# A hybrid encoder trunk on one core: float32 value and band products on halves of the array, and a new order of the head groups

## The chip, the cores and the metric

The kernel runs on one core of one Trainium2 chip. Its time is the device time of one execution in microseconds. The core has a matrix engine (TensorE; PE in the profile, its weight loads PEld), VectorE (DVE), ScalarE (ACT), GpSimd (POOL), and a queue that issues DMAs (SyncE, SP). TensorE reads SBUF and writes its results into PSUM, eight banks of 128 partitions x 512 float32.

## The reference

The input is x, 1024 tokens of 1024 channels in float32. Two layers are computed. Each normalises x, projects it with one matrix, and splits the columns among four groups of attention heads. Per layer:

```python
h = rms_norm(x, norm1_g[l])
proj = h @ w_in[l]
(a_cq, a_ckv, a_kr, b_q, b_k, b_v, c_q, c_k, c_v, d_q, d_k, d_v) = jnp.split(proj, splits, axis=-1)
y_a = mla_mixer(...)    # A: 4 heads, dense, keys of 64 + 32, from a low-rank latent
y_b = diff_mixer(...)   # B: 4 heads, dense, two softmaxes of keys of 32, p0 - lam * p1
y_c = swa_mixer(...)    # C: 4 query heads, 2 key heads of 64, keys within 128 tokens, with a sink
y_d = na_mixer(...)     # D: 4 heads of 64, a neighbourhood of 8 rows x 16 columns of the token grid
mix = jnp.concatenate([rms_norm(y_a), y_b, rms_norm(y_c), rms_norm(y_d)], axis=-1)   # gains left out here
x = x + mix @ w_out[l]
h = rms_norm(x, norm2_g[l])
x = x + jnp.square(jax.nn.relu(h @ w_up[l])) @ w_down[l]
```

After the layers x is normalised once more. All is float32, and so are the products as far as rounding goes: the kernel makes a float32 product out of three faster ones (below).

## The kernel before, in words

**Layout.** Everything is kept transposed: a tile has 128 channels on the partitions and the 1024 tokens along the row. Tokens go in halves of 512, a PSUM bank each.

**Split products.** A float32 operand is split into a high part, rounded to the reduced format float32r (ScalarE copies it, line 196), and a low part, the rest (a subtraction on VectorE or GpSimd, line 190). A product is then high x high + high x low + low x high, three matmuls in float32r (`passes`, lines 222 to 224). A projection of 128 channels is 2 halves x 8 blocks of inputs x 3 = 48 such matmuls.

**Stages of a layer** (`attention`, line 381). Two waves of projections make B's queries, keys and values (`several`, line 232). Then main streams of attention run, each with a fill beside it. `weave` (line 545) takes steps of the main stream and puts fill steps between them at a ratio; the main stream is emitted with a priority `lead`. The main streams and fills are, in order:

- B (`attn_b`, 871), with the latent projections of A and the projections of D as fill;
- D (`attn_d`, 1035), with the projections of C and the second, low-rank projections of A (`latent_up`, 698) as fill;
- C (`attn_c`, 1068), then A (`attn_a`, 931), both with the first half of the output projection for four of its eight tiles as fill (`groups_bd`, 472);
- the rest of the output projection (505 to 538).

Then comes the MLP (`mlp`, 1144), with an order of its own on TensorE; the change doesn't touch it. Queries, keys and values go through DRAM between projection and attention, written and read on SP's queue. A scheduler puts the emitted instructions of the attention stages in order on each engine, by its own model of durations and by the priorities; each engine then works strictly in that order.

**Dense attention** (A and B: `softmax`, 803, and `dense`, 818). For 128 queries: scores against all keys (line 810; B's three split passes are stacked along the contraction, 96 rows, and A needs three matmuls), a minimum on VectorE (812), exp on ScalarE (815). B combines two such tiles: a scaled copy on ScalarE (898) and a sum on GpSimd (899). For two query tiles at a time the probabilities are transposed on TensorE, four 128 x 128 blocks to a bank (846), and split into `pth` (ScalarE) and `ptl` (VectorE). The value product (834, 835) has as weights a tile of 64 high and 64 low channels of v, so that the upper half of the output is added to the lower one at the end (`pv_out`, 749). Per 128 keys there are two matmuls of 256 columns, one for `pth`, one for `ptl`.

**Banded attention** (C and D: `banded`, 966), one head at a time. Each of 8 query tiles meets the three key tiles around it. The score product is two matmuls in float32r over 128 rows, on which high and low parts are stacked (982). VectorE adds bias or mask and takes the minimum (1058, 1089), ScalarE takes exp (1061, 1092). Up to three blocks are transposed (991), split, and multiplied with v (1003, 1004), into a bank that was zeroed by a product (1032).

**After a group**: denominators are inverted, transposed, and sent through DRAM so that each row of a tile gets them (`denominators`, 761); the group is normalised and split for the output projection (`mix_b`, `mix_group`). These tails are generators; `tick` (774) takes a step of them now and then.

**Places.** In the attention stages PSUM is divided as mm 2 (products and small things), tr 2 (transposes), sb 3 (scores), pv 1 (value products); in the output projection all eight banks are mm.

Of the kernel before, what the change touches and what calls it, by code (L numbers as in the profile page):

```python
# [14 lines left out]
F = mybir.dt.float32  # L15
# [85 lines left out]
def layout(i):  # L101

    def padded(a, axis):
# [9 lines left out]
    wo = i["w_out"].reshape(n, 8, P, DM)[:, [2, 3, 6, 7, 4, 5, 0, 1]].reshape(n, DM, DM)  # L113
# [23 lines left out]
        + [col(i["out_g_" + s]) for s in ("mla", "swa", "na")]  # L137
# [10 lines left out]
class Trunk:  # L148
    def __init__(self, ctx, tc, d, out):
        self.ctx, self.tc, self.nc, self.d, self.out = ctx, tc, tc.nc, d, out  # L150
        self.ahead, self.tails = 4, deque()
# [117 lines left out]
    def rows_of(self, col, grid=False):  # L269

        n = col.shape[1]
        ps = self.bank("mm", [n, P])
        self.nc.tensor.transpose(ps, col, self.ident)
        sb = self.cp.tile([n, P], F, tag="rows", name="rows")
        self.nc.vector.tensor_copy(sb, ps)
        dr = self.dram.tile([n, P], F, tag="rows", bufs=4, name="drows")
        if grid:
            flat = dr.rearrange("a b -> (a b)").rearrange("(r b c) -> b r c", r=16, b=8)
            self.store(flat, sb.rearrange("b (r c) -> b r c", r=16))
        else:  # L280
            self.store(dr, sb)
        return dr
# [98 lines left out]
    def attention(self, l):  # L381
# [8 lines left out]
        qb, kb, vb = dr([2, 2, 4, 16, 2, S], "qb"), dr([2, 2, 4, 16, 2, S], "kb"), dr([4, P, 8, P], "vb")  # L390
        qd, kd, vd = dr([2, 2, P, S], "qd"), dr([2, 2, P, S], "kd"), dr([4, P, 8, P], "vd")
        qc, kc, vc = dr([2, 2, 2, 32, 2, S], "qc"), dr([2, 2, 32, 2, S], "kc"), dr([2, P, 8, P], "vc")
        lat, krd = dr([2, 3, P, S], "lat"), dr([2, 16, 2, S], "krd")
        qa = dr([2, 2, P, S], "qan"), dr([2, 4, 16, 2, S], "qar")
        ka, va = dr([2, 2, P, S], "kan"), dr([4, P, 8, P], "va")
# [13 lines left out]
        def proj_d():  # L409
            for t in range(2):  # L410
                yield from one(T_DQ[t], xs, self.ev_grid(rb, self.to_parts(qd[:, t], 0.125)))
                yield from one(T_DK[t], xs, self.ev_grid(rb, self.to_parts(kd[:, t])))
                yield from one(T_DV[t], xs, self.ev_grid(rb, self.to_values(vd[2 * t:2 * t + 2])))

        def proj_c():
            tabs = self.table("64", rb, nc.gpsimd)
            for t in range(2):
                yield from one(T_CQ2[t], xs, self.ev_rope(tabs, qc[:, t]))
            yield from one(T_CK, xs, self.ev_rope(tabs, kc))
# [4 lines left out]
        with ExitStack() as stack, ExitStack() as att:  # L424
            self.ap = att.enter_context(sbuf("att"))
            with self.banks(mm=2, tr=2, sb=3, pv=1):
                with sbuf("proj", "right") as self.pp:
# [35 lines left out]
                    self.tails.append(self.mix_b(mix, y["b"], self.gsub[:, l:l + 1]))  # L463
                    fill = chain(proj_c(), self.latent_up(l, lat, rows, qa, ka, va))
                    self.weave(self.attn_d(l, qd, kd, vd, y["d"]), fill, self.RD, self.LD, every=self.EV[1])
                gout = lambda n: self.gout[n][:, l]
                self.tails.append(self.mix_group(mix, 2, y["d"], gout("na")))
                wa = stack.enter_context(sbuf("wa", "right"))
                wo = stack.enter_context(sbuf("wo", "right"))
                sums, w_out = [], d["w_out"][l]  # L470

                def groups_bd():

                    for m in range(self.EARLY):
                        x = wo.tile([P, S], F, tag="sum", bufs=self.EARLY, name="sum")
                        self.load(x, saved[m])
                        sums.append(x)
                    while None in mix[:4]:
                        yield True
                    for m, x in enumerate(sums):  # L480
                        ws = self.weights(w_out[m, 0])
                        for n in range(2):
                            ps = self.mm_ps()
                            self.product(ps, ws, mix[:4], n)
                            sl = slice(n * 512, n * 512 + 512)
                            self.tt(x[:, sl], ps, x[:, sl], ALU.add)
                            yield True

                fill = groups_bd()
# [3 lines left out]
                self.tails.append(self.mix_group(mix, 6, y["a"], gout("mla"), nc.vector))  # L493
            with self.banks(mm=8):
# [9 lines left out]

                while None in mix[:6]:
# [84 lines left out]
    def ev_rope(self, tabs, dst):  # L590

        dst = dst.rearrange("a g f h s -> a (g f) h s")

        def ev(n, ps):
# [7 lines left out]
            self.emit_parts(t1, [(dst[:, :, h, sl].rearrange("a p s -> p a s"), slice(h * 64, h * 64 + 64))  # L602
                                 for h in range(2)])
# [30 lines left out]

    def to_values(self, dst, tag="mm"):
# [3 lines left out]
        def then(n, y):  # L639
# [3 lines left out]
            src = ps.rearrange("p (k h d) -> p h k d", k=4, h=2)  # L643
            b = self.both()
            v = b.rearrange("p h (k e) -> p h k e", k=4)
# [853 lines left out]
```

## Time and profile before

| | us |
|---|---|
| median of the 3 runs shown (lowest, highest) | 2697.52 (2692.25, 2699.81) |
| the profiled execution | 2692.41 |
| its span, from first to last instruction | 2690.6 |
| TensorE busy in it | 2545.8 |
| VectorE busy | 2014.2 |
| ScalarE busy | 1442.9 |
| GpSimd busy | 496.9 |

How to read it: an instruction group is named by the line of code that emits it, engine, operation, and out<-in by the program's own tile names. Lines 190 and 196 are those of the helpers that split, so there the tile names tell what is meant: `wl<-raw,wh` is a low half of weights, `ptl<-tr,pth` one of probabilities. A matmul's record lasts longer than its slot: the next one starts before it ends. Spacings of starts are therefore the price of a matmul in a stream, and durations its latency. PEclk is the share of its clock that TensorE was granted. In the table by stage, the figures behind "PE", "DVE" and so on are busy microseconds with the number of instructions, then the granted clock, the busy share of the DMA engines and GB/s.

### The profile page before, as it was taken

Reading aid. Unit: us, or ns where it says so; the run is one execution under the profiler, and the core shown is the slowest. Engines: PE = TensorE matmul, PEld = TensorE weight load, DVE = VectorE, ACT = ScalarE, POOL = GpSimd, SP = SyncE. Lnnn points to the kernel's source line nnn. Section 1 sums busy time; section 2 is a strip of 40 time slices with the busy share of each in tenths; the row PEclk is TensorE's granted clock in tenths of the full one; section 3 lists DMA queues with packets and bytes.
Section 4 is the critical chain, followed back from the end, with each engine's and each line's share of the span. In section 5 each row is a group of like instructions: output and inputs, shape, how many; then the busy total and the mean of one; then the engine's idle time right before and its main releaser. Section 6 shows DMA issues by size and latency. Waiting matters only on the chain.

```text
span 2690.6 us, 36835 instructions
## 1 busy us (share of the span) xinstructions
PE 2545.8 (95%) x12296; PEld 2107.6 (78%) x12296; DVE 2014.2 (75%) x3827; ACT 1442.9 (54%) x2601; POOL 496.9 (18%) x306
## 2 busy tenths in 40 slices
PE   8989988999899999999999999789998999999997
PEld 7778876787778887888877788678887788778886
DVE  6777867774977778888668777677749677788886
ACT  4667757664534444444437777576635344444444
POOL 2555642201000000000035556331010000000000
PEclk9999989999999999999999999889999999999998
DMA  5533598322144447444244446962221444664431
GB/s 169 177 106 123 160 282 254 83 88 60 51 154 143 161 162 269 146 141 141 96 136 140 121 118 174 306 200 70 70 71 61 152 152 151 227 221 150 132 102 63
DMA packets 186927, 389.15 MB, mean 145 GB/s; under 512 B 23712, under 2 KB 26736, under 8 KB 186736
## 3 DMA queue, kind: packets, MB, share of 16 engines
q1 hardware_dynamic: 172912, 361.62, 43.7%
q10 hardware_dynamic: 13824, 25.17, 2.6%
q8 instruction: 97, 1.59, 0.2%
q14 instruction: 94, 0.77, 0.1%
HBM read 263.29 MB, written 123.41 MB: 144 GB/s over the span
## 4 chain that ended last, share of the span: by engine, by line
PE 74%; DVE 12%; DMA 6%; ACT 4%; issue 3%; POOL 1%; SPq 0%; DVEq 0%; ACTq 0%; POOLq 0%
PE u L222 8%; PE u L224 8%; PE u L223 8%; PE mm L222 5%; PE mm L223 5%; PE mm L224 5%; PE p L222 5%; PE p L223 5%; PE p L224 5%; PE sb L810 3%; PE tr L846 2%; DVE p L812 2%; DVE part L190 2%; PE pv L835 2%; PE pv L834 2%
## 5 line engine op out<-in xcount | busy, mean ns | idle before, releaser
L196 ACT ACTIVATE wh<-raw 128x512 fp32r<-128x512 f32 x448 | 281.8, 630 | 595.9 <-PE u L223 336.0
L190 DVE TENSOR_TENSOR wl<-raw,wh 128x512 fp32r<-128x512 f32 x448 | 306.8, 685 | 76.9 <-ACT wh L196 75.6
L190 POOL TENSOR_TENSOR wl<-ws,wh 128x512 fp32r<-128x512 f32 (+1 forms) x112 | 146.5, 1310 | 1107.0 <-DMA saved<-x 664.1
L224 PE MATMUL u<-far,wl 128*128 128x512 f32 x768 | 302.4, 394 | 6.2 <-DVE wl L190 6.0
L222 PE MATMUL u<-far,wh 128*128 128x512 f32 x768 | 302.4, 394 | 3.3 <-ACT ev L1251 2.1
L223 PE MATMUL u<-far,wh 128*128 128x512 f32 x768 | 301.8, 393 | 0.9 <-DVE far L190 0.9
L190 DVE TENSOR_TENSOR ptl<-tr,pth 128x512 fp32r<-128x512 f32 (+2 forms) x384 | 238.3, 629 | 67.5 <-ACT pth L196 65.8
L815 ACT ACTIVATE p<-p,nm 128x1024 f32<-128x1024 f32 x192 | 220.1, 1147 | 91.1 <-DVE nm L812 89.6
L196 ACT ACTIVATE pth<-tr 128x512 fp32r<-128x512 f32 (+2 forms) x384 | 204.9, 546 | 104.4 <-PE tr L846 55.8
L222 PE MATMUL p<-far,wh 128*128 128x512 f32 x640 | 251.2, 393 | 2.6 <-DVE ev L190 2.6
L224 PE MATMUL p<-far,wl 128*128 128x512 f32 x640 | 250.0, 391 | 2.9 <-DVE wl L190 2.9
L223 PE MATMUL p<-far,wh 128*128 128x512 f32 x640 | 250.3, 391 | 0.0
L810 PE MATMUL sb<-stack 96*128 96x512 f32 x640 | 217.6, 421 | 18.8 <-DVE nm L812 17.8
L190 POOL TENSOR_TENSOR p<-p 128x1024 f32<-128x1024 f32 x64 | 154.0, 2410 | 141.4 <-ACT p L898 132.1
L190 DVE TENSOR_TENSOR raw<-raw 128x512 f32<-128x512 f32 x256 | 174.6, 686 | 6.7 <-DMA raw<-in_w_up 2.0
L224 PEld LDWEIGHTS u<-far,wl 128*128 128x128 f32 x768 | 145.8, 190 | 38.4 <-DVE wl L190 7.9
L222 PEld LDWEIGHTS u<-far,wh 128*128 128x128 f32 x768 | 146.1, 190 | 35.3 <-ACT ev L1251 2.9
L223 PEld LDWEIGHTS u<-far,wh 128*128 128x128 f32 x768 | 145.8, 190 | 31.9 <-DVE far L190 1.6
L222 PE MATMUL mm<-xh,wh 128*128 128x512 f32 x416 | 168.9, 406 | 1.3 <-DVE part L190 0.7
L812 DVE CUSTOM_DVE_ANT_0 p<-sb,zero,nm 128x512 f32<-128x512 f32 x192 | 142.4, 742 | 32.2 <-PE sb L810 28.6
L224 PE MATMUL mm<-xh,wl 128*128 128x512 f32 x416 | 166.5, 400 | 0.0
L223 PE MATMUL mm<-xl,wh 128*128 128x512 f32 x416 | 166.4, 400 | 0.0
(245 smaller groups left out, 5993.1 us busy)
## 6 DMA issues: line engine op xcount, KB each, us to landing
act<-acts SPq DMA_DIRECT2D x224, 256.0 KB
raw<-in_w_up SPq DMA_DIRECT2D x128, 256.0 KB
acts<-ev SPq DMA_DIRECT2D x128, 256.0 KB
raw<-in_w_down SPq DMA_DIRECT2D x128, 256.0 KB
acts<-ev ACTq DMA_DIRECT2D x96, 256.0 KB
ws<-in_w_in SPq DMA_DIRECT2D x76, 256.0 KB
rz<-drows SPq DMA_DIRECT2D x40, 256.0 KB
stack<-kd SPq DMA_DIRECT2D x32, 256.0 KB
```

What stands on the lines that cost most here:

```text
L190: (eng or self.nc.vector).tensor_tensor(out=out, in0=a, in1=b, op=op)
L196: nc.scalar.activation(hi, src, AF.Copy)
L222: mm(ps, w[0], x[0][:, sl], start=start, stop=False)
L223: mm(ps, w[0], x[1][:, sl], start=False, stop=False)
L224: mm(ps, w[1], x[0][:, sl], start=False, stop=stop)
L810: self.nc.tensor.matmul(ps, q[:, qt * P:(qt + 1) * P], k[:, sl], start=i == 0, stop=i == len(passes) - 1)
L812: self.nc.vector.tensor_tensor_reduce(out=p[:, sl], in0=ps, in1=self.zero[:, 0:1].bitcast(F).broadcast_to([P, 512]), scale=-scale, scalar= ...
L815: self.nc.scalar.activation(p, p, AF.Exp, bias=nm[:, 1:2], scale=-1.0, accum_out=z)
L834: nc.tensor.matmul(out, v[:, kt], h[:, sl], start=kt == 0, stop=False)
L835: nc.tensor.matmul(out, v[:, kt], lo[:, sl], start=False, stop=kt == 7)
L846: nc.tensor.transpose(t[:, k * 256 + i * P:k * 256 + (i + 1) * P], p[:, (j * 2 + k) * P:(j * 2 + k + 1) * P], self.ident)
```

## The change

**Value products in float32.** The transposed probabilities are copied once out of PSUM, unsplit, by ScalarE; in the stage of A and the bands ScalarE and VectorE take turns. v is kept as plain float32, 64 channels. A dense value product has 64 output rows: for even key tiles it writes partitions 0 to 63, for odd ones 64 to 127, and `pv_out` adds the halves as before. The eight products of a group of 256 queries are emitted in one go, after all four transposed tiles.

**Banded attention in float32, two heads at a time.** Two heads are stacked on the 128 partitions. Scores of one head use rows 0 to 63 of the array, those of the other rows 64 to 127; value products write 64 output rows each. Product results need no addition: one ScalarE copy takes them out (`pair_out`). C's key head and query head are paired anew, for which the host reorders C's rows of `w_out` and gains.

**B's combination** becomes one VectorE operation in place of ScalarE's copy and GpSimd's sum.

**Normalisation** of two heads shares one transpose and one way through DRAM (`normalise`).

**Order.** All projections, C's and A's second ones included, are fill beside B. Then A is the main stream, and D and C, in turn, its fill, with PSUM as mm 1, tr 2, sb 3, pv 2. The output projection stands whole after that.

```diff
-                    fill = chain(self.proj_latent(l, one, xs, rb, tabs, lat, krd, rows), proj_d())
+                    fill = chain(self.proj_latent(l, one, xs, rb, tabs, lat, krd, rows), proj_d(), proj_c(),
+                                 self.latent_up(l, lat, rows, qa, ka, va))
                     self.weave(chain.from_iterable(self.attn_b(l, t, qb, kb, vb, y["b"]) for t in range(2)),
                                fill, self.RB, self.LB, every=self.EV[0])
-                    fill = chain(proj_c(), self.latent_up(l, lat, rows, qa, ka, va))
-                    self.weave(self.attn_d(l, qd, kd, vd, y["d"]), fill, self.RD, self.LD, every=self.EV[1])
...
+            def bands():
+                yield from self.attn_d(l, qd, kd, vd, y["d"])
                 self.tails.append(self.mix_group(mix, 2, y["d"], gout("na")))
...
-                self.weave(self.attn_c(l, qc, kc, vc, y["c"]), fill, self.RC, end=False, every=self.EV[2])
+                yield from self.attn_c(l, qc, kc, vc, y["c"])
                 self.tails.append(self.mix_group(mix, 4, y["c"], gout("swa")))
-                self.weave(self.attn_a(l, qa, ka, krd, va, y["a"]), fill, self.RA, self.LA, every=self.EV[3])
+            self.turns = (True, False)
+            with self.banks(mm=1, tr=2, sb=3, pv=2), sbuf("band", "right") as self.bp:
+                self.weave(self.attn_a(l, qa, ka, krd, va, y["a"]), bands(), self.RA, self.LA, every=self.EV[1])
...
-    EV = (.5, .5, .7, 1)
-    EARLY, RC, RA, LA = 4, (8, 1), (3, 1), 0
+    EV = (.5, 1)
+    EARLY, RA, LA = 4, (17, 42), 40
-    NP, RB, RD, LB, LD = 6, (7, 8), (3, 2), 40, 50
+    NP, RB, LB = 6, (18, 41), 40
...
         def step(job, j):
...
-            h, lo = self.transposed(512)
-            self.split(h, lo, t)
-            ready.append((job, j, h, lo))
-            if len(ready) > 1:
-                product(*ready.pop(0))
+            ready.append(self.transposed(t))
+            if j == 3:
+                runs.append((job, list(ready)))
+                ready.clear()
+
+        def products():
+            job, pts = runs.pop(0)
+            probs, g, v, y, half, done = job
+            if g % 2 == 0:
+                self.pv = self.bank("pv")
+            out = self.pv[:, (g % 2) * 256:(g % 2) * 256 + 256]
+            for n, j in enumerate((3, 2, 1, 0)):
+                for k in range(2):
+                    nc.tensor.matmul(out[k * 64:(k + 1) * 64], v[:, j * 2 + k], pts[j][:, k * 256:k * 256 + 256],
+                                     start=n == 0, stop=n == 3)
...
+    def transposed(self, ps, pool=None, tag="pt", bufs=None):
+        t = (pool or self.ap).tile([P, 384 if pool else 512], F, tag=tag, bufs=bufs or self.NT, name="pt")
+        t = t[:, :ps.shape[1]]
+        if self.turns[0]:
+            self.nc.vector.tensor_copy(t, ps)
+        else:
+            self.nc.scalar.activation(t, ps, AF.Copy)
+        self.turns = self.turns[::-1]
+        return t
...
-                nc.scalar.activation(ps[1], ps[1], AF.Copy, scale=c)
-                self.tt(ps[0], ps[0], ps[1], ALU.add, nc.gpsimd)
+                nc.vector.scalar_tensor_tensor(out=ps[0], in0=ps[1], scalar=c, in1=ps[0], op0=ALU.mult, op1=ALU.add)
...
         def score(i):
...
-            for n, k in enumerate(ks):
-                mm(ps, qs[:, i * P:(i + 1) * P], k[:, keys], start=n == 0, stop=n == 1)
+            ps = [self.bank("sb")[:, :w] for _ in heads]
+            for b, r in zip(ps, heads):
+                mm(b, q[r, i * P:(i + 1) * P], k[r, lo * P:(hi + 1) * P], start=True, stop=True)
...
+        def products(pv, half, kbs):
+            for kb in kbs:
+                pts, i0, i1 = done[kb]
+                q0, q1 = max(i0, half * 4), min(i1, half * 4 + 3) + 1
+                for r, v, pt in zip(heads, vs, pts):
+                    mm(pv[r, (q0 - half * 4) * P:(q1 - half * 4) * P], v[:, kb], pt[:, (q0 - i0) * P:(q1 - i0) * P],
+                       start=False, stop=kb == 2 + 3 * half)
```

The helper functions that only carry data in the new layouts (`to_rows`, `to_values`, `vtile`, `ev_rope` with `whole`, the head loops of `attn_c` and `attn_d`) change with it and are not shown. `ahead`, the number of query tiles whose scores a band computes in advance, goes from 4 to 2.

More of the change, by code (lines that the diff above doesn't have):

```diff
@@ L469, in attention @@
[L469 to L487, printed above, removed]
@@ L765, in denominators @@
         yield
[L766 removed]
+        rz = self.rz_tile()
+        for j in range(2):
+            self.spread(rz[j * 64:(j + 1) * 64], rows, j, 2)
         yield
[L769 removed]
         self.tt(y, y, rz, eng=eng or self.nc.gpsimd)
@@ L867, in dense @@
             step(job, j)
-        product(*ready.pop(0))
+        while runs:
+            products()
         yield True
```

332 lines of the change are left out of this document (162 added, 170 removed).

## The prediction

> **What bounds the kernel now.** I read the page from the top: busy times, slices, chain.
>
> ```profile
> span 2690.6 us, 36835 instructions
> ...
> PE 2545.8 (95%) x12296; PEld 2107.6 (78%) x12296; DVE 2014.2 (75%) x3827; ACT 1442.9 (54%) x2601; POOL 496.9 (18%) x306
> ...
> PE   8989988999899999999999999789998999999997
> ...
> PEclk9999989999999999999999999889999999999998
> ...
> PE 74%; DVE 12%; DMA 6%; ACT 4%; issue 3%; POOL 1%; SPq 0%; DVEq 0%; ACTq 0%; POOLq 0%
> ```
>
> TensorE is busy 95% of the span and holds 74% of the chain: this is a TensorE kernel. Its few holes are places where the PE slice falls to 7 or 8 and the clock row drops with it. So I cut the span into stages (busy time by stage). Layer 0 runs from 0 to 696, its MLP to 1365, layer 1 from there to 2026. In each layer the rows are: first projections, B, D, C, then A with the output projection.
>
> ```profile
> core 0: us, PE busy (x) PEld busy (x) DVE busy (x) ACT busy (x) POOL busy (x), PEclk, DMA share, GB/s
> 0.00:109.00 109.00, 96.97 (x409) 78.16 (x410) 75.91 (x111) 50.49 (x78) 40.15 (x31) 0.94 0.61 196
> 109.00:330.00 221.00, 211.66 (x1152) 178.44 (x1151) 169.02 (x433) 161.65 (x263) 125.96 (x71) 0.98 0.41 119
> 330.00:415.00 85.00, 74.72 (x401) 63.58 (x400) 55.32 (x143) 53.33 (x132) 36.63 (x24) 0.90 0.97 287
> 415.00:509.00 94.00, 80.87 (x429) 62.66 (x428) 68.75 (x180) 64.28 (x155) 20.89 (x13) 0.96 0.56 173
> 509.00:696.00 187.00, 181.96 (x1031) 154.64 (x1032) 124.89 (x248) 102.59 (x180) 24.20 (x19) 1.00 0.26 75
> ...
> 1365.00:1437.00 72.00, 66.59 (x273) 53.28 (x272) 49.51 (x72) 28.21 (x49) 29.43 (x20) 0.91 0.62 179
> 1437.00:1651.00 214.00, 206.73 (x1131) 174.45 (x1129) 163.73 (x429) 160.64 (x261) 124.97 (x70) 0.98 0.41 119
> 1651.00:1740.00 89.00, 74.87 (x413) 64.76 (x410) 56.60 (x143) 53.66 (x132) 38.73 (x26) 0.92 0.97 281
> 1740.00:1838.00 98.00, 86.06 (x437) 68.92 (x436) 73.29 (x183) 64.93 (x157) 21.12 (x12) 0.88 0.55 170
> 1838.00:2026.00 188.00, 182.31 (x1033) 155.01 (x1034) 125.87 (x249) 102.99 (x181) 25.06 (x19) 1.00 0.25 74
> ```
>
> In the B and the A rows TensorE is idle for 3 to 4%. In the four D and C rows it is idle for 49.5 us (10.3, 13.1, 14.1, 11.9), 12 to 16% of each, and its clock is 0.88 to 0.96 there. D's row also has the DMA engines at 0.97, and the chain there runs over the latent loads:
>
> ```profile
> 1683.74 7.15 DMA rq<-drows
> 1690.91 9.87 DMA latp<-lat
> ```
>
> So there are two things to price: whether TensorE gets more or less to do, and whether those holes close.
>
> **TensorE's own work.** The pace of the present forms, from the spacing of starts in the order of time:
>
> ```profile
> 303.56 0.29 PE L834 MATMUL pv<-pth,v 128*128 128x256 f32 x1
> 303.68 0.28 PE L835 MATMUL pv<-ptl,v 128*128 128x256 f32 x1
> ...
> 305.09 0.39 PE L224 MATMUL mm<-xh,wl 128*128 128x512 f32 x1
> 305.32 0.39 PE L222 MATMUL mm<-xh,wh 128*128 128x512 f32 x1
> ...
> 35.76 1.95 PE L299 MATMUL mm<-ident,rs_r 128*128 128x128 f32 x16
> 37.46 0.48 PE L222 MATMUL pv<-xh,wh 128*128 128x512 f32 x1
> ...
> 1870.39 0.46 PEld L846 LDWEIGHTS tr<-ident,p 128*128 128x128 f32 x4
> ...
> L299 PE MATMUL mm<-ident,rs_r x64: 270/275/421, 35.8 to 2073.7; 128*128 128x128 f32 x64
> ...
> L1004 PE MATMUL pv<-ptl,v x160: 223/337/687, 365.0 to 1835.9; 128*128 128x256 f32 x64, 128*128 128x384 f32 x64, 128*128 128x128 f32 x32
> ```
>
> A split (float32r) product of 512 columns takes a slot of 0.23 us, one of 256 columns 0.117; on that line 384 columns are 0.172 and 128 are 0.062. L299 is the only plain float32 product with many columns: its 8 instructions leave 16 records, so each is two passes, and 16 in 1.70 us is 0.106 a pass. Is that the price of 128 columns, or of the weight load beside them? One pass lasts 270 ns at least; the split product of as many columns (L1004's shortest) lasts 223. The extra 47 ns is about one 128-column stream (0.055), so I read two cycles a column: a float32 instruction of 256 columns takes 0.424 alone, 384 takes 0.636, 128 takes 0.212. The lower bound (0.106 is the load alone) would be half of it.
>
> Removed, in both layers: 1024 value products of B and A, 1024 x 0.117 = 120; the bands' 320 value products, 128 x 0.172 + 128 x 0.117 + 64 x 0.062 = 41; the bands' scores, 192 x 0.172 + 64 x 0.117 = 40; 16 zeroing products, 4. Together 205 us.
>
> Added: 512 float32 value products, 217; the bands' 64, 64 and 32, 75; the bands' 128 scores, 75. Together 366 us if each runs alone, 183 if two always run side by side on the halves of the array (64 output rows each, or 64 input rows each). No run of before has two products on halves, so the pairing is a bound from both sides. I take pairing in order: the second pass of one instruction beside the first pass of the next. Then each unbroken run leaves one pass uncovered. In the changed program's order the 672 stand in 216 runs (58 full eights, but 44 lone scores: the scheduler puts transposes between). 216 x 0.27 = 59, so 183 + 59 = 242: **37 us more** than the 205 removed. By this term alone the change loses; gain can only come from the holes.
>
> **The other engines.** These rows carry the terms:
>
> ```profile
> L190 DVE TENSOR_TENSOR ptl<-tr,pth 128x512 fp32r<-128x512 f32 x256 | 173.2, 685 | 43.0 <-ACT pth L196 42.2
> L190 DVE TENSOR_TENSOR ptl<-tr,pth 128x384 fp32r<-128x384 f32 x96 | 52.0, 550 | 17.3 <-ACT pth L196 16.4
> L196 ACT ACTIVATE pth<-tr 128x512 fp32r<-128x512 f32 x256 | 148.0, 590 | 59.5 <-PE tr L846 55.8 <-DVE ptl L190 1.8 <-PE pv L834 0.2
> L898 ACT ACTIVATE p<-p,cb 128x1024 f32<-128x1024 f32 x64 | 72.9, 1144 | 12.2 <-DVE cb L897 10.3 <-DVE cb L896 0.8 <-DVE rs_r L255 0.7
> L190 POOL TENSOR_TENSOR p<-p 128x1024 f32<-128x1024 f32 x64 | 154.0, 2410 | 141.4 <-ACT p L898 132.1 <-PE mm L224 4.4 <-PE mm L222 4.0
> L200 DVE SCALAR_TENSOR_TENSOR xl<-x,par,xh 128x1024 fp32r<-128x1024 f32 x16 | 24.4, 1529 | 7.6 <-ACT xh L199 7.6
> L190 DVE TENSOR_TENSOR part<-mm,tabs 64x512 f32<-64x512 f32 x32 | 22.0, 688 | 0.5
> L190 DVE TENSOR_TENSOR part<-mm,tabc 128x512 f32<-128x512 f32 x16 | 11.0, 686 | 7.2 <-PE mm L224 3.9 <-PE mm L726 3.3
> L190 DVE TENSOR_TENSOR part<-mm,rkv 128x512 f32<-128x512 f32 x16 | 10.9, 683 | 2.2 <-PE mm L224 1.4 <-POOL both L190 0.7
> ```
>
> The low half on VectorE goes, 225 us and the step after the ScalarE copy with it (1.28 us per transposed tile become 0.6). B's scaled copy (1.14) and GpSimd sum (2.41) become one VectorE operation, at 1.53 by L200: 98 us. In stage A half the copies go to VectorE, 0.69 each for 64 and at most 0.55 for 64 banded ones: 79. VectorE loses 225 - 98 - 79 = 48 us net, ScalarE 73 and half of A's copies. GpSimd's B row loses 77 of its 126 us and takes on the low halves of the moved weights. One denominator transpose and DRAM trip now serves two heads, and values, D's and C's queries and keys go through DRAM once and not as two halves. None of these was on the path: TensorE's B row is 97% busy beside them. I count nothing for them; if TensorE should wait for VectorE in the new A stage, that is in the 11% below.
>
> **The stages, layer 1.** First projections: 72, unchanged. B takes over from D's row C's four projection tiles, 192 x 0.227 = 44, and the latent ones, 54 x 0.227 = 12, with some 24 transposes, 2: 58 us more on TensorE. Their weight loads, the latent loads and the stores go along on SP's queue, out of a row with the DMA engines at 0.97 into one at 0.41, so the 17 us of latent loads find other products in front. B: 214 + 58 = 272.
>
> A with D and C: A's scores 192 x 0.227 = 44, 432 transposes at a slot of 0.109 (0.46 us for four weight loads) 47, the float32 products 242/2 less B's 31 = 90, the rest 7: 188 us on TensorE. VectorE has 256 us in the D, C and A rows now; less 44 and 26 of low halves, plus 39 of copies, less the evacuations that move to B (the last three rows of the last fence, 44 in both layers, so 22) and the output's 24 sums at 0.69 (16), it has near 187 in the A stage and the output together, some 175 of it in the stage. ScalarE (222 in the three rows, less the same copies) stays below. So TensorE is first, VectorE close behind, and **the cover is gone**: up to now independent projections stood beside every group (D and C still lost 12 to 16%, A beside the output projection 3%); now A and the bands have only each other. A product that waits at the head of TensorE's queue holds the other group's transposes too, and with two transpose banks for both, the VectorE and ScalarE copies behind. I take a loss of 11%, between the A row and the D and C rows: 208.
>
> Output projection: 384 x 0.227 = 87, alone, plus 8 for the hand-over, 95. A's tail runs beside the first 240 of these products (54 us), so it costs nothing unless it is longer than they are.
>
> Sum: 72 + 272 + 208 + 95 = 647 against 661. Layer 0: 109 + 279 + 208 + 95 = 691 against 696. The MLP is untouched. Together -19 us on the profiled execution, which took 2692.4 us, 1.8 beyond its span and 5 below the median of the runs shown: **2674 us**. With the A row's 3% loss it would be 2644, with D's 16% 2704; that is the forecast's own range, both signs in it.
>
> **Rivals.**
>
> (1) *The halves don't overlap* (ends slower). Then the float32 products take 366, not 242: 124 us more, 23 of it in each B stage, 39 in each A stage. TensorE would have 227 us in stage A, far ahead of the other engines, so of the loss there only some 13 remain in place of 20: 2674 + 124 - 14, and 12 less for B's present idle time (17 us in both layers), = 2772. For it: no row shows any overlap. Against it: no row either. It ends slower than before as soon as a fifth of the second passes stays uncovered (the 18 us of gain are a fifth of the 98 between the two cases). The Trainium skill (TensorE: Matmul & The Clock Gate, section on packing small matmuls) gives 2.38 times for three column tiles; by it the 366 would be about 230. No run here shows that.
>
> (2) *Each change between halves and whole array waits for the array to empty.* A 512-column product lasts 0.39 while the next starts after 0.23: 0.16 us are normally hidden. The 216 runs have some 420 edges; 0.16 each is 67 us, none of it hidden by another engine: 2741. For it: 44 lone scores between transposes. Against it: only that no trace has such an edge. The Trainium skill (TensorEngine Tiling (Array Packing), Key Properties) says that changing the mode drains TensorE; by that rule this rival is the time. No row here can say.
>
> (3) *Both passes of a pair run side by side and the holes close.* Then 183, no uncovered pass, and A's 3%: 2644 - 59 = 2585, and with half of that 2615. Faster.
>
> (4) *The change doesn't do what it says*: A waits for the latent values at the hand-over from B, since they are now the last of the fill, the way D's row waited for 17 us. 17 us in each layer: 2708.
>
> **How the numbers follow.** Forecast 0.42, (1) 0.27, (2) 0.15, (3) 0.10, (4) 0.06. About 0.3% (8 us) is what a measurement can tell from no change. The forecast's range gives 0.30 faster, 0.06 same, 0.06 slower; (3) is faster; (1) and (2) slower; (4) 0.02 same, 0.04 slower. Faster 0.40, same 0.08, slower 0.52. The range reaches over (4) and (2) to just past (1), and down to the half-way case of (3): 2612 to 2776. It leaves out half of (3) and the upper half of what (1) could be.
>
> **What would show it.** In the new trace the float32 value products start every 0.21 us per instruction inside a run of eight (forecast), every 0.42 (rival 1), or 0.11 (rival 3). The first start after a run comes 0.16 us late under rival 2. The A stage is near 208 us with TensorE above 85% and VectorE next. B lasts about 275 with TensorE at 95% or more, and no DMA chain at its end. Wrong would be: B bound by VectorE's new sums, or TensorE's clock below 0.9 through stage A.

## The result, and the profile after

The changed kernel takes **2741.07 us** (2735.18 to 2745.17), the kernel before 2698.22 beside it: ratio 1.0161, interval 1.0137 to 1.0186, so 43 us slower. The forecast was 2674, on the faster side. First the page of the changed kernel: span, busy times, the slices of TensorE and of its clock.

```profile
span 2739.3 us, 35471 instructions
...
PE 2599.4 (95%) x12264; PEld 2000.2 (73%) x12264; DVE 1892.8 (69%) x3531; ACT 1296.2 (47%) x2373; POOL 325.5 (12%) x222
...
PE   8999989998989998999999998999999999999997
...
PEclk9999999998999999999999999999999999999998
```

The other engines got lighter, as intended: VectorE by 121 us, ScalarE by 147, GpSimd by 171. TensorE got heavier by 54, and it was already the bound. The 7 inside the row of slices, where D's group stood in layer 1, is gone and the clock dips less often; yet the time went up. Cut into stages (rows: first projections, B, A with the bands, output projection, MLP; then layer 1 and its MLP):

```profile
0.00:112.00 112.00, 96.13 (x403) 76.41 (x404) 75.02 (x115) 50.21 (x78) 33.87 (x28) 0.94 0.58 178
112.00:395.00 283.00, 268.37 (x1368) 198.96 (x1367) 181.41 (x420) 145.55 (x260) 85.05 (x59) 0.97 0.45 134
395.00:609.00 214.00, 206.85 (x1189) 129.51 (x1187) 123.34 (x347) 124.83 (x285) 9.47 (x4) 0.98 0.28 80
609.00:723.00 114.00, 103.76 (x441) 82.95 (x440) 53.00 (x81) 38.00 (x68) 34.38 (x23) 0.91 0.28 82
723.00:1390.00 667.00, 648.36 (x2852) 532.59 (x2852) 526.84 (x815) 300.33 (x504) 9.75 (x6) 0.99 0.45 146
1390.00:1466.00 76.00, 68.49 (x270) 52.73 (x269) 50.33 (x79) 28.47 (x50) 23.87 (x18) 0.89 0.57 163
1466.00:1750.00 284.00, 267.81 (x1370) 197.78 (x1369) 180.92 (x419) 145.59 (x260) 85.79 (x59) 0.98 0.45 134
1750.00:1965.00 215.00, 207.46 (x1194) 130.14 (x1192) 123.78 (x348) 124.78 (x286) 9.46 (x4) 0.98 0.28 80
1965.00:2073.00 108.00, 98.84 (x440) 79.98 (x441) 53.72 (x81) 38.12 (x68) 33.89 (x23) 0.95 0.26 81
```

| stage, layer 0 / layer 1 | forecast | measured |
|---|---|---|
| first projections | 109 / 72 | 112 / 76 |
| B and all projections | 279 / 272 | 283 / 284 |
| A and the bands | 208 / 208 | 214 / 215 |
| output projection | 95 / 95 | 114 / 108 |

Two things are to be seen. The stage of A and the bands is nearly right in length, but for another reason: TensorE is busy 207 of its 214 us (97%), where the forecast had 188 of 208. And the output projection, 384 products that need 87 us, is the stage that is furthest off, with a clock of 0.91.

**Inside the A stage.** A part of TensorE's order of time in that stage; a float32 instruction leaves two records, so x16 is a run of eight products, x2 a single half.

```profile
480.27 1.94 PE L872 MATMUL pv<-pt,v 128*64 128x256 f32 x14
482.14 0.66 PE L857 MATMUL tr<-ident,p 128*128 128x128 f32 x4
482.73 0.65 PE L872 MATMUL pv<-pt,v 128*64 128x256 f32 x2
483.30 0.66 PE L857 MATMUL tr<-ident,p 128*128 128x128 f32 x4
...
487.56 1.95 PE L872 MATMUL pv<-pt,v 128*64 128x256 f32 x16
489.44 0.76 PE L1014 MATMUL tr<-ident,p 128*128 128x128 f32 x5
```

From its start to the start behind it the run of eight takes 1.88 us. In experiment 1, where the eight stand one after the other, it takes 3.60; so the halves do run side by side. In the single records of this trace the two halves of a pair start 0.007 us apart and the next pair 0.209 later. The price is at the ends: four transposes between two groups of halves take 0.59 (482.14 to 482.73) where four slots of 0.109 are 0.44, and the lone half takes 0.57 where its two passes are 0.43. That is **0.15 us for each change between halves and whole array** (0.094 before the first instruction of the new mode and 0.052 behind it, in the records). The trace has 418 changes of mode, 14 of them between the two kinds of halves (64 output rows, 64 input rows), which cost as much: 418 x 0.146 = 61 us. Without them the products and scores on halves take 241 us in all.

**Inside the output stage.** The rows of one tile (duration min/median/max, first and last start) and then stretches of that stage, 609 to 618 and on:

```profile
L193 POOL TENSOR_TENSOR yd<-yd,rz x4: 2342/2408/2417, 545.6 to 621.0; 128x1024 f32<-128x1024 f32 x4
...
L369 ACT ACTIVATE sq<-yd x2: 1043/1044/1046, 549.8 to 553.8; 128x1024 f32<-128x1024 f32 x2
```

```profile
609.00:618.00 9.00, 7.76 (x33) 6.40 (x32) 1.68 (x6) 1.28 (x4) 0.00 (x0) 0.63 0.32 89
618.00:639.00 21.00, 16.38 (x66) 12.05 (x65) 9.92 (x13) 5.58 (x8) 10.36 (x5) 0.91 0.25 64
639.00:652.00 13.00, 11.33 (x46) 9.36 (x47) 3.58 (x8) 2.80 (x8) 5.82 (x6) 0.75 0.21 63
652.00:668.00 16.00, 13.54 (x54) 10.24 (x54) 5.80 (x6) 5.51 (x8) 6.93 (x5) 0.94 0.38 91
668.00:723.00 55.00, 54.75 (x246) 44.90 (x245) 32.02 (x49) 22.83 (x41) 11.27 (x10) 0.99 0.27 89
```

D's group was squared by 555 and then lay still for some 60 us: the last of its products on GpSimd starts at 621.0, after the A stage. The tails advance by one step (a tick) for each step of A, A has 17 steps, and D's, C's and B's remaining tails want more than that. So D's last, C's whole and A's tail run one behind the other in the output stage. Until 668 TensorE is busy 49 of 59 us at a clock between 0.63 and 0.94; then it runs full.

### The profile page after: what moved, and what is told of

It reads as the page before. It is cut to its first block, busy times and chain, and to the rows that moved or that the text cites. A ratio compares the mean times of both kernels' runs of the same rounds, so it can differ in the third digit from the quotient of the medians.

```text
span 2739.3 us, 35471 instructions
## 1 busy us (share of the span) xinstructions
PE 2599.4 (95%) x12264; PEld 2000.2 (73%) x12264; DVE 1892.8 (69%) x3531; ACT 1296.2 (47%) x2373; POOL 325.5 (12%) x222
## 5 line engine op out<-in xcount | busy, mean ns | idle before, releaser
L193 POOL TENSOR_TENSOR wl<-ws,wh 128x512 fp32r<-128x512 f32 (+1 forms) x112 | 156.1, 1397 | 1061.6 <-ACT wh L199 1013.7
L823 ACT ACTIVATE pt<-tr 128x512 f32<-128x512 f32 (+2 forms) x256 | 140.0, 558 | 164.0 <-PE tr L857 99.3
L857 PE MATMUL tr<-ident,p 128*128 128x128 f32 x1024 | 168.2, 281 | 14.9 <-DVE p L926 9.5
L857 PEld LDWEIGHTS tr<-ident,p 128*128 128x128 f32 x1024 | 121.2, 142 | 65.5 <-issue 18.9
```

Of the source, the lines that this page charges most:

```text
L193: (eng or self.nc.vector).tensor_tensor(out=out, in0=a, in1=b, op=op)
L823: self.nc.scalar.activation(t, ps, AF.Copy)
L857: nc.tensor.transpose(t[:, k * 256 + i * P:k * 256 + (i + 1) * P], p[:, (j * 2 + k) * P:(j * 2 + k + 1) * P], self.ident)
```

## The experiments

Ratios are to the kernel before, with the 95% interval.

| version | us | ratio |
|---|---|---|
| the change | 2741.07 | 1.0161 [1.0137, 1.0186] |
| all products on one half | 2821.78 | 1.0452 [1.0429, 1.0474] |
| runs of two | 2786.44 | 1.0318 [1.0291, 1.0345] |
| runs kept whole, nothing else | 2729.93 | 1.0136 [1.0116, 1.0156] |
| tails early | 2700.84 | 1.0005 [0.9995, 1.0016] |
| order alone, split products | 2816.43 | 1.0431 [1.0415, 1.0447] |
| order alone, tails early | 2777.01 | 1.0293 [1.0269, 1.0317] |
| dense float32 products, B's combination and normalisation, old order | 2711.95 | 1.0051 [1.0032, 1.0070] |
| tails early, bands split | 2695.67 | 0.9997 [0.9985, 1.0010] |
| tails early, even fill | 2749.84 | 1.0196 [1.0181, 1.0211] |
| tails early, bands split, even fill | 2752.65 | 1.0208 [1.0194, 1.0222] |
| tails early, runs kept whole | 2693.65 | 0.9978 [0.9965, 0.9992] |
| tails early, runs whole, even fill | 2722.83 | 1.0088 [1.0065, 1.0111] |
| tails early, runs whole, bands split, even fill | 2717.27 | 1.0069 [1.0046, 1.0091] |
| tails early, runs whole, bands split | 2694.54 | 0.9990 [0.9980, 1.0000] |

**1. Do the halves overlap?** All dense products go to one half.

```diff
-out[k * 64:(k + 1) * 64], ..., start=n == 0, stop=n == 3
+out[0:64], ..., start=n == 0 and k == 0, stop=n == 3 and k == 1
```

> Edit of the changed kernel: all eight dense value products of a run write the same 64 output rows, so that two can never be side by side; the addition of the halves goes. Theory (TensorE bounds B and A, and the halves overlap fully: in the changed kernel's trace two products start 6 ns apart and the next two 209 ns later): 512 products take 0.427 us in place of 0.213, +109 us, some 10 of it into idle time: 2835 to 2850. Rival (the new A stage is bound by its softmax chain, and the overlap is worth little): under +40, below 2780.

Measured +81 us against the change, less than the 94 to 109 expected and far above the rival. The row is seven products, for which the change has 1.94:

```profile
483.92 3.24 PE L870 MATMUL pv<-pt,v 128*64 128x256 f32 x14
```

The overlap is real: without it the change would have lost 123 us, not 43.

**2. What does a change of mode cost?** The pair of products is put behind each block of transposes; the same products, but 699 changes of mode in place of 419.

```diff
-            if j == 3:
-                runs.append((job, list(ready)))
+            if len(ready) > 1:
+                products()      # one pair
```

> Edit of the changed kernel: each pair of dense value products is emitted after the transposes of the next pair, as before, and not in runs of eight. In the order of instructions the changes between half and whole array go from 419 to 699. Theory (each such change waits until the array is empty, 0.094 us more than a start in a stream, and nothing hides it): +26 us, 2762 to 2772. Rival (the changes cost nothing that counts; what costs is the order of the groups): within 8 us of 2741.

Measured +45 us, above the range: the expectation knew of 0.094 for each of the 280 changes, and the 0.146 read above gives 41. The trace also has 29 more halves that stand alone, which at 0.22 each are another 6.

**3. Are the tails the loss in the output stage?**

```diff
-    EV = (.5, 1)
+    EV = (.5, 3)
```

> Edit of the changed kernel: three steps of the groups' tails for every step of stage A in place of one. In the changed kernel D's and C's normalisations end only after A, in the output projection, where TensorE idles for 10 us a layer and runs at a lower clock. Theory (the output projection waits for these tails): the output stage of 114 and 108 us comes near 95, so -25 to -30 us, 2711 to 2720. Rival (it waits for its own weights, or the tails take the same time from stage A): within 8 us of 2741.

Measured -40 us: this one number brings the change back to the time before. The output row of this version, and its D tile:

```profile
606.00:703.00 97.00, 94.34 (x435) 76.42 (x435) 48.24 (x72) 33.98 (x61) 24.12 (x19) 1.00 0.24 74
```

```profile
L193 POOL TENSOR_TENSOR yd<-yd,rz x2: 2362/2364/2365, 515.2 to 517.5; 128x1024 f32<-128x1024 f32 x2
```

D's last product starts at 517.5 in place of 621.0. From A's last value product to the last product of the output projection the stage takes 92.6 and 91.8 us in place of 114.1 and 108.1, so 38 of the 40 us lie there (the row's stretch of 97 us is some 4 us wider than that). The clock came back too: the granted share is 1.00, and the products that start every 0.43 us at 613 to 618 of the change are gone. More came than expected because the stage fell below the 95 us that the expectation took as its end.

**4. The order alone.** The new order of groups with before's split products, in other places of the memory where they needed it.

```diff
-fill = chain(self.proj_latent(...), proj_d())
+fill = chain(self.proj_latent(...), proj_d(), proj_c(), self.latent_up(...))
...
+self.weave(self.attn_a(...), bands(), self.RA, self.LA, every=self.EV[1])
```

> Edit of the kernel before: only the order of the change (all projections beside B, A beside D and C, the output projection alone), with the float32r split products, one banded head at a time and B's combination as they were. Bands get places of their own. Theory (the order closes D's and C's holes, and what costs is the float32 products' edges and lone scores): stage A 170 us of TensorE work and little idle, B as in the changed kernel, output 108 to 114: near 2665, faster than before. Rival (the order itself loses): 2720 or more.

The theory fell: +118 against before. The order does not carry the gain; it carries the loss, and what the change adds to the order takes 75 us of it back. That is the float32 products together with B's merged combination, the two heads of a band at a time and the shared normalisation. Early tails in this version:

> The new order with the split products of before, as in the run with the order alone, and three ticks of the normalisation tails to each step of A in place of one. It asks whether the order's loss of 118 us (2816 against 2698) is the late tails or the order itself. The output stage lasted 139 us in each layer of the order alone, and 97 in the whole change with early tails, at the same TensorE work (104 and 94 us busy). Theory: the tails are most of it, 2 x (139 - 97) = 84 us go, so 2732 (2720 to 2745). Rival: VectorE (162 of 205 us busy in the stage of A and the bands there) and GpSimd (163 of 298 in B's) have no room, the tails only move into the stage of A, and it stays above 2780.

Measured -39, the same as in the change, and half of what was expected. Both theories were half right: the output stage fell from 137 and 138 us to 92 in both layers (from A's last value product to the last product of the output), which is the 84 and more of the theory, and the stage of A and the bands grew from 207 and 209 to 234 and 232, which is the rival. Stretches of B and of A with the bands in this version:

```profile
112.00:411.00 299.00, 267.01 (x1347) 215.89 (x1346) 194.39 (x476) 183.29 (x299) 162.81 (x97) 0.93 0.50 155
411.00:617.00 206.00, 179.57 (x1060) 150.96 (x1060) 156.02 (x405) 143.38 (x328) 17.61 (x7) 0.94 0.46 121
```

B has 267 us of TensorE where the change has 268, and takes 299 us in place of 283; the A stage (whose end slid to 645) has TensorE at 87%, where the order with late tails has 92%.

So TensorE's busy time is nearly the same either way, and what the split version loses is waiting. With late tails 52 of the 75 us lie in the output stage, behind the tails; they have five steps for two heads in the split version and three in the change. With early tails the difference is 76 us (2777 to 2701), and lies in the stage of A and the bands (40) and before it (34). In that A stage TensorE is idle for 29 us in layer 0 in place of 10, and 18 of them are waits for the split copies on VectorE and ScalarE. In B's stage it is idle for 32 in place of 15; 7 of them are waits for split copies and 6 for GpSimd's sum in B's combination. What each part of the change is worth here was not separated.

In the old order, where other work stood beside every group, the dense products were tried. This version also has B's merged combination and the shared normalisation:

```diff
-mm(pv, v[:, kt], h, ...); mm(pv, v[:, kt], lo, ...)     # split, B and A
+runs of eight float32 products, B and A; bands and order as before
```

> The order of before, with D beside the projections and C and A beside the output's early half, and only the dense products of B and A in float32, in runs of eight; the banded groups keep their split products. Theory: TensorE's own work is the same either way (266.5 us split and 267.3 float32 in B's stage), and before had only its D and C stages with holes, which these edits do not touch: 2688 to 2710, no change to speak of. Rival: what the float32 products take off VectorE, ScalarE and GpSimd (about 110, 150 and 170 us in all) is what made them worth 75 us inside the new order, and it pays here too: 2660 or less.

Measured +14: just above the theory's range. The profiled execution loses ahead of A, in D's and C's stages, which the theory took as untouched: in layer 0 TensorE is idle there for 35 us in place of 23. A and the output behind the bands' last score take 11 us less, both layers together. So +14 without the order, +118 for the order alone, +43 together.

**5. Which part of the float32 products pays?** The bands go back to split products, in the new order with early tails.

```diff
-q[r, ...], k[r, ...]     # one head on each half, float32
+qs, ks[0], ks[1]         # one head at a time, two split passes
```

> The whole change with early tails, but the banded groups D and C keep the split products and split scores of before (one head at a time, whole array, no modes); only A and B have float32 products in runs of eight. TensorE was busy 188.8 us in the stage of A and the bands with everything split, and 202.4 with everything float32, while B's stage has 266.5 and 267.3: so the 14 us lie in the bands. Theory: a stage that is 95% TensorE gives most of them back, 10 to 13 in each layer, so 2701 - 2 x 11 = 2678 (2672 to 2686), faster than before and than the change. Rival: the splits of the D and C projections return to B's stage, which took 298 to 301 us with everything split against 282 to 284, and eat it: 2698 or more.

Measured 2695.67, 5 below the version with everything float32, with intervals that overlap: not told apart from the version before it. The A stage got 11 us shorter in layer 0 and 6 in layer 1, but B's got 2 and 3 longer, part of what the rival had. So the bands' float32 products pay nothing that can be told. The step from the order with early tails and split products (2777) to this version is 81 us, by nearly the same edits that cost 14 in the old order.

**6. A version that beats both?** In B's stage the last stretch, where the fill is the thin latent products, is the weak one. The rows are of the version with early tails:

```profile
112.00:310.00 198.00, 194.44 (x961) 147.18 (x959) 114.94 (x264) 88.11 (x156) 55.50 (x38) 0.98 0.33 96
310.00:394.00 84.00, 72.82 (x399) 50.72 (x397) 66.66 (x159) 55.81 (x103) 28.65 (x20) 0.92 0.73 228
```

```diff
-                ev(n, ps)
-                yield True
+                ev(n, ps)
+            yield True          # one step for two groups of products
-    RB = (18, 41)
+    RB = (18, 34)
```

> The whole change with early tails, and the latent up-projections beside B handed out two groups of products at a time (34 steps of fill in place of 41, ratio 18 to 34), so that the thick D and C projections reach further into B. It asks where the 283 us of B's stage, 11 more than the sum had, come from. In its first 198 us TensorE is busy 98%, in the last 84 us, where the fill is the thin latent products, 87% (72.8 us) at a granted clock of 0.92. Theory: the thin fill leaves B's own softmax chain uncovered, and some 5 to 8 of the 11 us of each layer go: 2701 - 2 x 6.5 = 2688 (2682 to 2692), below before. Rival: the last stretch waits for its DMAs (0.73 of their time busy) or for the latent values whatever lies beside it, and nothing goes: 2697 to 2705.

> The same handing out of the fill, on the version whose banded groups keep their split products (2695.7). Theory: 2 x 6.5 us go here too, 2683 (2676 to 2689), and the two gains add, so this is faster than the kernel before by 0.3 to 0.8%. Rival: 2693 or more.

Both lost, by 49 and 57 us. The stretch did fill:

```profile
310.00:400.00 90.00, 82.69 (x422) 56.95 (x420) 66.70 (x147) 51.25 (x95) 32.12 (x22) 0.96 0.65 197
```

But in the new order of instructions 98 value products on a half stood alone in place of 42, with 497 changes of mode in place of 393. An edit to the fill had broken up runs that it never touched. So the next edit holds the runs together:

```diff
+            with self.tc.high_priority(offset=100):
                 for n, j in enumerate((3, 2, 1, 0)):
                     for k in range(2):
                         nc.tensor.matmul(...)
```

> The whole change with early tails, and the eight dense products of a run given a priority of their own, so that nothing else is put between them: runs that stand alone as a single half fall from 42 to 14, whole runs of eight rise from 56 to 68, and changes between half and whole array from 393 to 333. Theory: a change costs 0.09 to 0.16 us and a lone half 0.21 us, so 60 x 0.09 to 0.16 = 5 to 10, and 28 x 0.21 = 6, go: 2701 - 13 = 2688 (2684 to 2692), below before. Rival: with the runs first, B's and A's scores come later and VectorE's softmax with them, and the gain goes into holes: 2697 or more.

> The same priority for the runs, with the evenly handed fill that lost 49 us. That version had closed the holes it aimed at (16 us less between the transposes' starts), but its order of instructions had 98 single halves in place of 42 and 497 changes in place of 393, and the value products, the bands' scores and the projections took some 50 us longer from start to start. With the runs kept it has 16 single halves and 349 changes. Theory: the broken runs were the loss, and the closed holes remain: 2701 - 16 - 7 - 5 = 2673 (2668 to 2685). Rival: the loss was the fill itself, thick projections next to the bands' first scores, and it stays at 2720 or more.

> The same priority and the same fill, with the banded groups in split products: all 64 runs are runs of eight, and no half stands alone (61 did). Theory: 2753 falls below the 2696 of the split bands with the old fill, by the holes (16) and by the 20 single halves that it had (4): 2676 (2668 to 2686). Rival: 2710 or more.

The first came out at 2693.65, 7 us below the version with early tails: half of the sum, and 0.2% below the kernel before with an interval that leaves 1 out, though less than the 0.3% that the prediction set as the bound. The other two got back 27 and 35 us, far from what was expected. Whole runs bring the even fill's loss from 49 to 29 us, and from 57 to 23 with split bands, so broken runs were two and three fifths of it.

The rest lies behind B's stage. With whole runs the even fill makes the way from B's first score to the bands' first one 9 us shorter, both layers together, and the A stage 31 us longer. The bands' scores, from start to next start, take 96 us there and 70 without it, and half of the difference is waits right behind them. Layer 0 of the version with whole runs and the even fill, in order of time (in brackets the idle time before) and as stretches:

```profile
402.20 1.65 PE L1003 MATMUL sb<-bk,bq 64*128 64x384 f32 x2
408.64 3.15 PE L268 MATMUL mm<-pairs,rz 128*128 128x2 f32 x14 [4.80 <-ACT rz L940]
...
403.00:409.00 6.00, 1.20 (x4) 0.36 (x2) 0.57 (x2) 1.47 (x3) 2.34 (x1) 0.50 0.36 114
409.00:418.00 9.00, 9.00 (x29) 6.21 (x28) 1.69 (x5) 4.26 (x14) 0.00 (x0) 0.50 0.00 0
```

The next instruction on TensorE is a sum of B's own normalisation, and it waits 4.8 us for ScalarE's square (3.7 in layer 1); until 418 the granted clock is 0.50. So here, too, TensorE stands behind a tail. No run moved this tail alone, so how much of the 29 us it accounts for is not shown.

The same edit in the change itself, and with split bands:

> The change itself, with only the eight dense products of a run kept together: single halves 42 to 14, changes between half and whole array 419 to 361, tails as late as in the change. Theory: it brings what the bounds of the expectation for the early tails were, 58 x 0.09 = 5 and 28 x 0.21 = 6, so 2741 - 11 = 2730 (2726 to 2735). Rival: with early tails the same edit gave 7 (2701 to 2694), half of that sum, because the runs then wait in the place of the scores: 2734 to 2738. Nothing at all (2739 or more) would say that single halves fall into time that the stage loses anyway.

> The version with early tails and split products in the banded groups (2695.7), with the dense runs kept together: single halves 20 to 2, 62 whole runs of 64. Theory: 18 x 0.21 = 4 and some changes of mode go, 2690 (2686 to 2693), the fastest version here, 0.3% below before. Rival: the runs delay the scores as much as they save, 2695 or more.

In the change it is worth 11 us, as summed with 0.09 for each change; with the 0.146 read above the sum is 14.5. In both traces with whole runs A's and B's scores take 12 to 16 us more from start to next start than without, so part of the gain goes back into waits, as the rivals had it. With the bands split the edit gives 1: that version had few broken runs. Nothing here beats the kernel before by more than 0.2%.

## Why the prediction was wrong, step by step

**The step that failed** is the output stage: "A's tail runs beside the first 240 of these products (54 us), so it costs nothing unless it is longer than they are". It is not A's tail alone. The change leaves A's 17 steps as the only ticks for D's, C's and A's tails, and the output needs D's values first. The diff had the numbers (the tails advance by the edited rate, one a step); the prediction did not count ticks against steps. The two output stages cost 32 us more than the 190 forecast, and early tails alone take 40 us off the whole, 38 of them in these stages.

**TensorE's work** is the second step that failed, by a term that was put at nothing: the changes of mode, 61 us in this trace, which rival (2) had at 67. Without them 242 us were forecast for the float32 instructions on halves and they take 241, but that is luck. The forecast set the second pass of one product beside the first of the next, which leaves one pass uncovered in each run; in the trace both passes of a pair run side by side (1.73 for eight, the lower bound), and what is left over comes from halves and scores that stand alone. The sum also divides the 366 us among 672 instructions, where with the scores they are 512 + 160 + 128 = 800: a pass is then 0.23 and not 0.27, and the same rule gives 232. So the 37 us of more work were 97. The time rose by only 43, and TensorE's busy time by 54, because the instructions that went had taken some 295 us from start to next start in the kernel before, waits included, and not the 205 of their slots: most of the 97 stands where waits had been. By stage, 148 changes stand in each stage of A and the bands (22 us) and 60 in each of B (9 us). Rival (2)'s price (0.16) and its count (420) held (0.146 and 418). That its 2741 is the measured time to the us is luck: the forecast below it missed the tails, and had a loss that did not come. The rule of the Trainium skill that was weighed there (TensorEngine Tiling (Array Packing), Key Properties: a change of mode drains the array) agrees with these rows; it gives no price, and the runs give 0.15 us.

**The 11% in the A stage** did not come: TensorE is busy 97% there, a loss of 7 us and not 20 in each layer. The cover that the bands and A give each other was enough in this version. With split products the same order has 92% there, and 87% with early tails, most of it waits for the split copies (experiment 4): the risk was real, but for another version. VectorE, which the step put close behind TensorE with some 175 us in that stage, has 123 there; the sum left 12 us for it in the output stage, where it has 53. In the A stage two errors nearly cancel: 22 us of mode changes that were not counted, 13 of waiting that did not come, and the stage is 6 to 7 longer than forecast. By stages the 67 us between 2674 and 2741 are 32 in the output projections, 16 in B, 13 in A and the bands, 7 in the first projections, and 1 less in the rest. The experiments give 40 of them to the tails and 11 to broken runs; the other 16 were not won back by a run that changed one thing, though tails and whole runs together reach 2694.

**The holes of D and C** closed, as forecast, and **B** took 283 and 284 where 279 and 272 were forecast: its TensorE work was only 3 us more than the 265 of the sum, but 15 us were idle and not 7, most of it in the last stretch of thin fill (experiment 6).

**The other engines**: "I count nothing for them" came out for the old order and fails as a habit: nearly the same edits cost 14 us beside other work, and are worth 81 in the new order with early tails (2777 to 2696). B's merged operation was 1.41 us each (forecast 1.53).

```profile
L926 DVE SCALAR_TENSOR_TENSOR p<-p,cb 128x1024 f32<-128x1024 f32 x64 | 90.1, 1408 | 1.3
L821 DVE COPY pt<-tr 128x512 f32<-128x512 f32 x64 | 44.0, 688 | 26.2 <-PE tr L857 26.2
```

**The rivals.** (1) is out: experiment 1 shows the overlap. (2) is in, as one of two causes. (3) is half in: pairs overlap fully, the holes of D and C closed, but modes and tails ate it. (4) is out: between 112 and 609 TensorE's longest waits for a load are 1.5 and 1.4 us, and both are of the bands' queries and keys. Of the signs named, 0.21 us for each product of a run was seen; rival (3)'s sign of 0.11 was badly put, since full overlap also gives 0.21 for an instruction (0.108 for a record). What tells them apart are the single records: the passes of two halves start 0.007 us apart, up to the last pair of a run.

## What to carry to other kernels

When a change removes the steps that drive deferred work, count steps against ticks before costing its tail at nothing: here one number in a rate was worth about what the whole change had lost. Instructions on halves of the array want long unbroken runs: count the changes of mode in the scheduled order, not in the source, and hold a run together explicitly, since an edit elsewhere can break it. And price load on other engines by what stands beside them: nearly the same edits were worth 81 us in one order and cost 14 in another.

## What the runs showed of the hardware

A change between halves and whole array costs 0.146 us in either direction, 0.094 in front of the new mode's first instruction and 0.052 behind it; runs of two gave 0.16 a change, with the halves that came to stand alone in it. Two float32 products on the two halves start 0.007 us apart and run fully side by side; the Trainium skill (TensorE: Matmul & The Clock Gate, Measured speedup vs the span model) has some 4 ns for each tile; the trace agrees in kind, with 7 ns.

The clock fell at the hand-over to the output stage: TensorE does narrow sums there for 1.95 us and waits for 1.24, and the products behind them start 0.43 us apart, later every 0.23.

```profile
609.02 1.95 PE L268 MATMUL mm<-ones,sq 128*128 128x1 f32 x16
...
613.02 0.63 PE L226 MATMUL mm<-mixl,wh 128*128 128x512 f32 x1
...
613.45 0.63 PE L227 MATMUL mm<-mixh,wl 128*128 128x512 f32 x1
...
618.39 0.39 PE L227 MATMUL mm<-mixh,wl 128*128 128x512 f32 x1
...
618.62 0.40 PE L225 MATMUL mm<-mixh,wh 128*128 128x512 f32 x1
```

The stretch from 609 to 618 has a granted clock of 0.63, that from 639 to 652 has 0.75; with early tails the whole stage has 1.00. In experiment 6 it was 0.50 from 403 to 418 us, around a wait of 4.80 us. What of the light work or the waits lowers it was not tested.
